# Seven products instead of eight for the gates and for half of u, with the tokens' sums stored ahead

## The chip, the core and the metric

The kernel runs on one core of a Trainium2 chip. The core has five engines that each work through their own list of instructions in order: TensorE (PE in the profile), VectorE (DVE), ScalarE (ACT), GpSimd (POOL) and SyncE (SP, which here issues DMA transfers). They meet only at semaphores. The metric is the device time of one execution in microseconds (us), the median of several runs.

## The reference

The kernel computes one decoder block for 2048 tokens of 1024 channels, all in float32:

```
h    = rmsnorm(x)
proj = h @ w_in                     # 1024 -> 5376 columns
q, k, v = rope(..), rope(..), ..    # 12 heads of 64
u, z = gelu(..), gelu(..)           # 512 columns each
gate_a, gate_b = sigmoid(..), ..    # 1024 columns each
y_attn = dilated_attention(q, k, v) # 3 groups x 4 heads; softmax over the groups' log-sums
y_gmlp = u * (spatial(layernorm(z)))
y = (gate_a * (y_attn @ wa) + gate_b * (y_gmlp @ wg)) @ w_out
x = x + rmsnorm(y)
x = x + rmsnorm(relu(rmsnorm(x) @ w1)**2 @ w2)
```

The change concerns `proj` alone: the 2048 columns of the two gates for all tokens, and the 512 columns of u for the first 1024 tokens.

## The kernel before, in words

A float32 product is made of three products of numbers of fewer bits: each operand is split into a high part (a rounded copy) and a low part (the difference), and `mm3` (lines 95 to 97) adds high x high, high x low and low x high in one bank of PSUM. `split` (lines 70 to 78) makes the two parts: the high part is a copy on ACT (or POOL, line 72), the low part a subtraction on DVE. A "step" is the smallest piece of projection work that is placed by hand: one k block of 128 channels, three matmuls with 512 tokens in their free axis.

The tokens are four chunks of 512, chunks 0 and 1 being half 0, chunks 2 and 3 half 1. The program has these stages. The first part normalises x, transposes it into hT (`prenorm_cols`) and makes v, q and k. hT of two chunks lies in SBUF at a time (high and low, 4 MB for both): while the first part works on chunks 2 and 3, hT of 0 and 1 goes to memory in DRAM as `hT_d` and is read back later by `reload_h`. Then come u and z of half 1, and then the gates, of half 1 first and of half 0 after it. The gates' steps are the filler for attention: 48 attention units (three groups of 16) need PE for some 3 us each, in four short bursts that wait for other engines (scores; transposes of the exponentials; probabilities times v; transposes of the result), and between the bursts the main loop calls `steps(n)`, which takes n steps from the generator `filler`. In an attention unit ACT makes the exponentials (`e`, L585), copies the transposed ones out of PSUM (`ph` L610, `pf` L618) and copies the result (`pvs` L626); DVE subtracts the row maximum and takes the sums (`nm` L582, `o` L631). `att` holds the unnormalised results with their row sums.

When the last unit is through, `combine` joins the three groups, chunk by chunk: it loads A (L639), takes the maximum M, the exponentials E (L647) and the weights, multiplies (L659), adds (L661, L662, on DVE for the first chunk and POOL for the others), transposes on PE (`yt`, L667) and copies out. `steps(30)`, 20, 17 and 13 of filler stand ahead of the four transposes. Then u and z of half 0 are made, the two branches and the gates are merged, and the MLP follows, whose first matrix product (L994) is already done by Strassen's seven products, with the sums of its weights made on POOL (L965 to L968) from the raw tiles `w1r`, of which it holds five.

Nothing is scheduled by a planner around the change: each engine's order is the order of the program text as the generators interleave it, and every tile has a fixed number of buffers, for which the next user waits. SP's queue, too, is in order: a DMA that waits for a buffer or for its data holds back all those behind it.

## Time and profile before

| | us |
|---|---|
| three runs | 2790.17, 2791.38, 2792.4 (median 2791.38) |
| the profiled execution, its span | 2791.02, 2789.3 |
| first part (v, q, k), until | 431.6 |
| u of half 1, until | 475.3 |
| z of half 1, until | 525.8 |
| gates, attention units from 548.5, last unit's transposes at | 1017.7 |
| combine and u of half 0, until | 1098.8 |
| z of half 0, until | 1145.9 |
| branches and merge, until | 1493.9 |
| MLP | 2779 |

The stage times are starts of PE's instructions in the timeline. The profile shows for each instruction its engine, line, output and input tiles, shape, duration, and the idle time of its engine just ahead of it with what ended it. Matmuls are pipelined: one of 512 columns is shown with 0.39 us, but a new one starts about every 0.23 us, and that spacing is what counts. The mean granted clock of TensorE is 0.99 of full speed over the span.

### The profile page before, as it was taken

To read this page: it belongs to the slowest core of one execution; us is meant where nothing else is said; L and a number is where in the kernel's file an instruction comes from. 1 tells how busy PE (TensorE), PEld (TensorE's weight loads), DVE (VectorE), ACT (ScalarE), POOL (GpSimd) and SP (SyncE) were. 2 spreads that over 40 slices of the span, in tenths; PEclk is the share of its full clock that TensorE was granted. 3 is DMA by queue.
4 is the path that set the end of the run, shared out by engine and by line. 5 is a ranking of instruction groups with operands and counts; after the bars stand their busy time and mean duration, and the time that the engine had idled before them with its cause. 6 is when DMAs were issued, how large, how long until landed. Compare 5 with 4: busy or idle time off the path is not lost. (4 is left out here: it accounts for less than half of the span.)

```text
span 2789.3 us, 36260 instructions
## 1 busy us (share of the span) xinstructions
PE 2720.9 (98%) x13412; PEld 2282.3 (82%) x13412; DVE 1545.3 (55%) x2643; ACT 1053.1 (38%) x2151; POOL 945.3 (34%) x777
## 2 busy tenths in 40 slices
PE   8999999999989999999998999999999999999998
PEld 8889888988878888887787788788887887777787
DVE  5664562344443344564556644555436777777766
ACT  4212111144444321354444554555444333233334
POOL 0241341200000014312315432323214666777645
PEclk9999999999999999999999999999999999999999
DMA  7545446366666645555657544554343122222236
GB/s 256 177 147 165 155 148 198 113 190 197 193 204 195 195 162 163 158 193 163 185 181 250 169 117 129 170 178 121 109 143 114 54 83 84 83 83 84 83 104 213
DMA packets 298386, 426.10 MB, mean 153 GB/s; under 512 B 18528, under 2 KB 172384, under 8 KB 298208
## 3 DMA queue, kind: packets, MB, share of 16 engines
q1 hardware_dynamic: 210512, 372.64, 41.9%
q10 hardware_dynamic: 87696, 51.13, 6.1%
q8 instruction: 106, 1.74, 0.3%
...
## 5 line engine op out<-in xcount | busy, mean ns | idle before, releaser
L1534 PE MATMUL ya<-T_spots,s 128*128 128x512 f32 x1272 | 313.3, 392 | 4.7 <-DVE acc L1542 2.7
L1534 PEld LDWEIGHTS ya<-T_spots,s 128*128 128x128 f32 x1272 | 239.1, 188 | 59.1 <-issue 4.5
L70 ACT ACTIVATE s<-sraw 128x768 fp32r<-128x768 f32 (+1 forms) x184 | 126.2, 696 | 358.3 <-POOL sraw L1333 199.3
L994 PE MATMUL aa<-B,A 128*128 128x512 f32 x768 | 187.1, 396 | 6.8 <-ACT xs L1008 4.5
L78 DVE TENSOR_TENSOR s<-sraw,s 128x512 fp32r<-128x512 f32 x171 | 163.7, 980 | 34.8 <-ACT s L70 33.2
L994 PEld LDWEIGHTS aa<-B,A 128*128 128x128 f32 x768 | 145.3, 190 | 40.8 <-ACT xs L1008 4.9
L965 POOL TENSOR_TENSOR s<-w1r 128x512 f32<-128x512 f32 x32 | 43.1, 1348 | 395.5 <-DVE S L78 335.1
L72 POOL TENSOR_SCALAR w_g<-w_g_r 128x1024 fp32r<-128x1024 f32 x32 | 33.6, 1050 | 412.5 <-PE g L97 330.1
L1534 PE MATMUL yc<-T_spots,s 128*128 128x512 f32 x624 | 164.3, 394 | 3.6 <-POOL T_spots L78 3.6
L95 PE MATMUL x<-hT_a,wq 128*128 128x512 f32 x384 | 149.7, 390 | 0.0
L97 PE MATMUL x<-hT_a,wq 128*128 128x512 f32 x384 | 149.4, 389 | 0.0
L96 PE MATMUL x<-hT_a,wq 128*128 128x512 f32 x384 | 149.4, 389 | 0.0
L1534 PEld LDWEIGHTS yc<-T_spots,s 128*128 128x128 f32 x624 | 115.9, 188 | 33.7 <-POOL T_spots L78 9.7
L631 DVE TENSOR_REDUCE o<-po 128x256 f32<-128x512 f32 x48 | 33.2, 691 | 183.5 <-PE po L630 183.5
L78 POOL TENSOR_TENSOR T_spots<-w2r,T_spots 128x512 fp32r<-128x512 f32 x86 | 123.2, 1458 | 5.4 <-ACT T_spots L70 5.4
L70 ACT ACTIVATE hl<-r 128x512 fp32r<-128x512 f32 x48 | 30.4, 634 | 231.4 <-POOL r L276 86.7
L95 PE MATMUL g<-hT_b,w_g 128*128 128x512 f32 x256 | 105.6, 412 | 0.0
L95 PE MATMUL o<-wo,mg 128*128 128x512 f32 x256 | 100.9, 394 | 4.1 <-ACT mg L70 4.1
L95 PE MATMUL g<-hT_a,w_g 128*128 128x512 f32 x256 | 104.5, 408 | 0.0
L793 POOL TENSOR_TENSOR g<-g,g 128x512 f32<-128x512 f32 x28 | 38.8, 1385 | 185.7 <-DVE g L791 185.6
L70 ACT ACTIVATE S<-w1r 128x512 fp32r<-128x512 f32 x96 | 60.1, 630 | 110.0 <-PE ac L994 63.8
L97 PE MATMUL g<-hT_a,w_g 128*128 128x512 f32 x256 | 100.8, 394 | 0.0
...
## 6 DMA issues: line engine op xcount, KB each, us to landing
...
sraw<-sd SPq DMA_DIRECT2D x128, 256.0 KB, 3.4
qk<-hl SPq DMA_DIRECT2D x24, 1024.0 KB, 5.3
...
w2r<-in_w_mlp_out_dram SPq DMA_DIRECT2D x16, 1024.0 KB, 6.6
```

What stands on the lines that cost most here:

```text
L70: act.activation(hi, src, AF.Copy)
L72: pool.tensor_scalar(hi, src, 1.0, 1.0, op0=OP.mult, op1=OP.mult)
L78: (pool if lo_eng == "pool" else dve).tensor_sub(lo, src, f32(hi))
L95: pe.matmul(ps, lh, rh, start=start, stop=False)
L96: pe.matmul(ps, lh, rl, start=False, stop=False)
L97: pe.matmul(ps, ll, rh, start=False, stop=stop)
L631: dve.tensor_reduce(ot[:, :, j * 64:(j + 1) * 64], po.rearrange("p (b h e) -> p b e h", b=4, h=2), axis=AX.X, op=OP.add)
L793: (dve if dt == KT - 1 else pool).tensor_add(parts[0], parts[0], parts[1])
L965: pool.tensor_add(s1, a21, a22)
L994: pe.matmul(p, w[:, l, k, :], h[:, r, k, :], start=i in (1, 6, 5) and not k and not n, stop=k == 3 and n == 2, skip_group_check=True)
L1534: pe.matmul(p, s[:, l], w[:, r], start=i in (1, 2, 5) and not m and not o, stop=m == 1 and o == 2, skip_group_check=True)
```

## The change

The gates' weights are taken as pairs: 256 columns (two blocks f of 128), 1024 channels (two halves), against a half's 1024 tokens (two chunks). Such a pair is a 2 x 2 by 2 x 2 block product. Before it was 8 block products of 4 steps; now it is 7, by Strassen's scheme in Winograd's form, for the 16 gate pairs (those of half 1 first, then those of half 0) and for the two pairs of u of half 0. A pair has thus 28 steps (84 matmuls) where it had 32 (96). The A operands are the weights and their sums (A11, S2, A12, S3, S1, A22, S4), the B operands the tokens and their sums (B11, T2, B21, T3, T1, T4, B22), in this order of use.

- The sums of the tokens T1 to T4 are made in the first part: for each of the odd chunks and each block of 128 tokens, two reads of the even chunk's h from `h_d`, four subtractions on POOL, and one store into `t1_d`. ACT's extra copy of each transposed block, which half the chunks had, is now made for all.
- The sums of the weights are made pair by pair: one raw tile `wr` of 1 MB (one buffer) is loaded, four POOL operations over 128 x 512 make S1, S3, S2 and S4 in place, and each of the seven operands is split by ACT and DVE into one of four places of `A_room`. `prepare(m + 4)`, which does this for the operand of the product four places later, stands behind product m.
- The products' results are joined with two ACT copies (xs and c1) and five DVE additions a pair.
- Operands of half 1 lie in SBUF as they come from the first part (B) or are read ahead of the gates (T). During the last pair of half 1 each operand of half 0 takes the place of the one just used: `load_op`, two loads of 512 KB, two high parts on ACT and two low parts on DVE of 128 x 1024, 14 of each in place of `reload_h`'s 8.
- 16 gate pairs and 2 u pairs are 504 steps, where there were 576. The loop over attention units gives each unit 8 steps up to unit 25 and 9 later (it was 9 throughout), `combine` gets 24, 14, 9 and 5 steps. u and z of half 1 are now complete, with their `sz_out`, before the tiles of attention are opened.

The rows below are from the engines' lists of instructions: in brackets what a row waits for, x the count of like rows.

**SP's queue behind z of half 1, before.** `ygd` is the store of the spatial gating's result, `ur` the read of u that belongs to it, `w_g_r` the raw weights of a gate.

```order
L91 DMA w_g_r_4799<-in_w_in_dram 128x1024 [waits DMAHW7_49,DMAHW6_49,DVE_49]
L421 DMA ygd<-sb_4514 128x512 [waits Pool_49]
L421 DMA ygd<-sb_4525 128x512 [waits DMAHW0_49,Pool_49]
L414 DMA ur_4668<-ud 128x512 [waits DMAHW4_49,DMAHW1_49]
L414 DMA ur_4679<-ud 128x512 [waits DMAHW5_49,DMAHW2_49]
L91 DMA w_g_r_4804<-in_w_in_dram 128x1024 [waits DMAHW3_49,DVE_49]
L91 DMA w_g_r_5085<-in_w_in_dram 128x1024 [waits DMAHW6_49,DVE_49]
L479 DMA gated<-gt_4637 128x512 [waits Activation_49]
L91 DMA w_g_r_5090<-in_w_in_dram 128x1024 [waits DMAHW3_49,DVE_49]
```

**The same place now**; `wr` is a pair's raw weights, `gated` the store of a gate.

```order
L436 DMA ygd<-sb_4613 128x512 [waits DMAHW7_49,Pool_49]
L522 DMA wr_4700<-in_w_in_dram 128x2048 [waits DMAHW0_49,PE_49]
L429 DMA ur_4768<-ud 128x512 [waits DMAHW4_49,DMAHW1_49]
L436 DMA ygd<-sb_4756 128x512 [waits DMAHW2_49,Pool_49]
L429 DMA ur_4779<-ud 128x512 [waits DMAHW6_49]
L436 DMA ygd<-sb_4767 128x512 [waits Pool_49]
L429 DMA ur_4790<-ud 128x512 [waits DMAHW5_49,DMAHW1_49]
L436 DMA ygd<-sb_4778 128x512 [waits Pool_49]
L542 DMA gated<-c_2_4823 128x512 [waits DMAHW7_49,Activation_49]
L522 DMA wr_4842<-in_w_in_dram 128x2048 [waits DMAHW0_49,DVE_49]
L436 DMA ygd<-sb_4789 128x512 [waits Pool_49]
```

The first weights of the gates, which were asked for between the stores and waited only for their own buffer, are now one load of 1 MB that waits for PE (the tile lies where the weights of z were, which z's last matmul reads) and stands behind a store that waits for POOL; the second pair's waits for the first's low parts on DVE.

**ACT in one attention unit of the first group, before.** `gt` is the copy of a finished gate block.

```order
L477 ACTIVATE gt_5270<-g_5181 128x512 [waits DMAHW5_49,PE_49]
L610 ACTIVATE ph_5257<-pT_5252 128x512 [waits PE_49,Activation_49]
L585 ACTIVATE e_5223,o_4834<-e_5223,nm_5238 128x256 [waits DVE_49]
L585 ACTIVATE e_5223,o_4834<-e_5223,nm_5238 128x256 x3
L610 ACTIVATE ph_5265<-pT_5260 128x256 [waits PE_49,Activation_49]
L618 ACTIVATE pf_5268<-pT_5260 128x256 [waits DVE_49]
L626 ACTIVATE pvs_5301<-pv_5292 128x512 [waits PE_49,Activation_49]
```

**ACT in such a unit now**; the tile `A_room` receives the high parts of a pair's seven operands.

```order
L737 ACTIVATE ph_5708<-pT_5703 128x512 [waits PE_49,Activation_49]
L712 ACTIVATE e_5674,o_5383<-e_5674,nm_5689 128x256 [waits DMAHW2_49,DVE_49]
L70 ACTIVATE A_room<-wr_5657 128x512 [waits DMAHW7_49]
L712 ACTIVATE e_5674,o_5383<-e_5674,nm_5689 128x256 x3
L737 ACTIVATE ph_5716<-pT_5711 128x256 [waits PE_49,Activation_49]
L70 ACTIVATE A_room<-wr_5657 128x512 [waits PE_49,Pool_49]
L745 ACTIVATE pf_5719<-pT_5711 128x256 [waits DVE_49]
L753 ACTIVATE pvs_5749<-pv_5740 128x512 [waits PE_49,Activation_49]
L70 ACTIVATE A_room<-wr_5657 128x512 [waits PE_49]
```

Where a copy that waits for PE alone stood, there are now high parts. The first in these rows waits for the load of the next pair's raw tile and stands ahead of three exponentials and of `ph`; the second waits for POOL's sums and stands ahead of `pf` and `pvs`.

**DVE behind the last unit's sum, before**: the combine's first rows follow it at once (w_u is a filler weight).

```order
L631 TENSOR_REDUCE o_8545<-po_9132 128x4x64 [waits PE_49]
L78 TENSOR_TENSOR w_u_0_9408<-w_u_r_9409,w_u_0_9408 128x1024 [waits DMAHW0_49,Pool_49]
L78 TENSOR_TENSOR w_u_1_9413<-w_u_r_9414,w_u_1_9413 128x1024 [waits DMAHW2_49,Pool_49]
L642 TENSOR_TENSOR M_9148<-A_9144 128x16 [waits DMAHW1_49,DMAHW0_49]
L643 TENSOR_TENSOR M_9148<-M_9148,A_9144 128x16 [waits DMAHW2_49,DVE_49]
L646 TENSOR_TENSOR E_9151<-A_9144,M_9148 128x4x4 [waits DVE_49]
L646 TENSOR_TENSOR E_9151<-A_9144,M_9148 128x4x4 x2
L650 TENSOR_TENSOR Z_9156<-E_9151,A_9144 128x4x4 [waits Activation_49]
```

**DVE at the same place now**, starting three rows behind the last `o<-po`; `u_115`, `xs` and `u_113` are outputs of the first u pair, `w_z` the weights of z of half 0.

```order
L78 TENSOR_TENSOR A_room<-wr_9341,A_room 128x512 [waits PE_49,Activation_49]
L572 TENSOR_TENSOR u_115_9599<-xs_9548,s_113_9552 128x512 [waits DMAHW5_49,DVE_49,PE_49]
L78 TENSOR_TENSOR w_z_0_9453<-w_z_r_9454,w_z_0_9453 128x1024 [waits DMAHW7_49,Pool_49]
L78 TENSOR_TENSOR w_z_1_9458<-w_z_r_9459,w_z_1_9458 128x1024 [waits DMAHW6_49,DMAHW0_49,Pool_49]
L578 TENSOR_TENSOR u_115_9599<-u_115_9599,s_116_9608 128x512 [waits DVE_49,PE_49]
L769 TENSOR_TENSOR M_9480<-A_9476 128x16 [waits DMAHW2_49,DMAHW1_49]
L581 TENSOR_TENSOR xs_9548<-xs_9548,s_113_9552 128x512 [waits DMAHW6_49,PE_49]
L78 TENSOR_TENSOR w_z_0_9463<-w_z_r_9464,w_z_0_9463 128x1024 [waits DMAHW3_49,Pool_49]
L584 TENSOR_TENSOR u_113_9565<-u_113_9565,s_116_9608 128x512 [waits PE_49]
L78 TENSOR_TENSOR w_z_1_9468<-w_z_r_9469,w_z_1_9468 128x1024 [waits DMAHW4_49,Pool_49]
L770 TENSOR_TENSOR M_9480<-M_9480,A_9476 128x16 [waits DMAHW5_49,DVE_49]
L773 TENSOR_TENSOR E_9483<-A_9476,M_9480 128x4x4 [waits DVE_49]
```

Ahead of the first chunk's maximum M, or between its two halves, there are now four low parts of `w_z`, one of `A_room`, and four additions of the first u pair, which wait for PE's products.

The diff, cut to its core:

```diff
--- before.py
+++ after.py
-    hT_d = dtile([2, P, KT, 512], "hTd")
+    h_d = dtile([3, P, KT, 512], "hd")
+    t1_d = dtile([2, P, 4, 4, 512], "t1d")
...
     def prenorm_cols(c, i):
+        half, odd = c // 2, c % 2
         if i == 0:
-            hT[c] = hp.tile([P, 2, KT, 512], F32R, name=f"hT_a{c}", tag="hT", bufs=2)
-        h, xt = hT[c], xts.pop((c, i))
-        for k in range(0, KT, 4):
+            H[c] = [hp.tile([P, 2, 4, 512], F32R, name=f"B{n + 1}{odd + 1}_{half}", tag=f"B{n + 1}{odd + 1}") for n in range(2)]
+        xt, isl = xts.pop((c, i)), slice(i * P, (i + 1) * P)
+        raw = xp.tile([P, 5, 4, P], F32, name=f"tr_{c}{i}", tag="tr", bufs=2)
+        if odd:
+            for n in range(2):
+                sp.dma_start(raw[:, 3 * n], h_d[c - 1, :, 4 * n:4 * n + 4, isl])
+        for n in range(2):
+            k = 4 * n
...
-            hh, hl = (h[:, o, k:k + 4, i * P:(i + 1) * P] for o in range(2))
+            hh, hl = (H[c][n][:, o, :, isl] for o in range(2))
             p3 = pt.rearrange("p (k t) -> p k t", k=4)
             act.activation(hh, p3, AF.Copy)
             dve.tensor_sub(hl, p3, f32(hh))
-            if c < 2:
-                raw = xp.tile([P, 4, P], F32, name=f"hr_{c}{i}{k}", tag="hr", bufs=3)
-                act.activation(raw, p3, AF.Copy)
-                sp.dma_start(hT_d[c, :, k:k + 4, i * P:(i + 1) * P], raw)
-    def reload_h(c):
-        hT[c] = hp.tile([P, 2, KT, 512], F32R, name=f"hT_b{c}", tag="hT", bufs=2)
-        for k in range(0, KT, 2):
-            split_in(hT[c][:, :, k:k + 2], hT_d[c, :, k:k + 2, :], None, "act")
+            to = raw[:, 2 + 2 * n if odd else n]
+            act.activation(to, p3, AF.Copy)
+            if c < 3:
+                sp.dma_start(h_d[c, :, k:k + 4, isl], to)
+        if odd:
+            pool.tensor_sub(raw[:, 0], raw[:, 2], raw[:, 0])
+            pool.tensor_sub(raw[:, 1], raw[:, 4], raw[:, 0])
+            pool.tensor_sub(raw[:, 2], raw[:, 4], raw[:, 2])
+            pool.tensor_sub(raw[:, 3], raw[:, 3], raw[:, 1])
+            sp.dma_start(t1_d[half].rearrange("p o k t -> p (o k) t")[:, :, isl],
+                         raw[:, :4].rearrange("p o k t -> p (o k) t"))
...
+    SEVEN = ((1, "A11", "B11"), (6, "S2", "T2"), (2, "A12", "B21"), (7, "S3", "T3"), (5, "S1", "T1"), (4, "A22", "T4"),
+             (3, "S4", "B22"))
+    pairs = [(13 + n, gate_d, n, 1) for n in range(8)] + [(13 + n, gate_d, n, 0) for n in range(8)]
+    pairs += [(9, u_d, 0, 0), (10, u_d, 1, 0)]
+    ops = {}
+    def load_op(half, name):
+        pl = hp if name[0] == "B" else tp
+        w = pl.tile([P, 2, 4, 512], F32R, name=f"{name}_b{half}", tag=name)
+        if name[0] == "T":
+            src = t1_d[half, :, int(name[1]) - 1]
+        else:
+            k = 4 * (int(name[1]) - 1)
+            src = h_d[2 * half + int(name[2]) - 1, :, k:k + 4]
+        for k in (0, 2):
+            split_in(w[:, :, k:k + 2], src[:, k:k + 2], None, "act")
+        ops[half, name] = w
+    def seven():
+        seq = [(p, *t) for p in pairs for t in SEVEN]
+        room = hp.tile([P, 2, 4, 512], F32R, name="A_room", tag="B12")
+        left, raws = {}, {}
+        def prepare(m):
+            if m >= len(seq):
+                return
+            pair, i, name, _ = seq[m]
+            wi = pair[0]
+            if name == "A11":
+                raws["t"] = ap.tile([P, 2560], F32, name=f"wr_{m}", tag="wr")
+                sp.dma_start(raws["t"][:, :2048], a["w_in"][wi].rearrange("p k c -> p (k c)"))
+            t = raws["t"]
+            q = t[:, :2048].rearrange("p (k c) -> p k c", c=256)
+            a11, a12, a21, a22 = (q[:, k:k + 4, f:f + P] for f in (0, P) for k in (0, 4))
+            s1 = t[:, 2048:].rearrange("p (k c) -> p k c", c=P)
+            w = room[:, :, m % 4].rearrange("p o (k c) -> p o k c", k=4)
+            split(w[:, 0], w[:, 1], dict(A11=a11, S2=a11, A12=a12, S4=a12, S3=a21, S1=s1, A22=a22)[name])
+            left[m] = w
+            if name == "A11":
+                pool.tensor_add(s1, a21, a22)
+                pool.tensor_sub(a21, a11, a21)
+                pool.tensor_sub(a11, s1, a11)
+            elif name == "A12":
+                pool.tensor_sub(a12, a12, a11)
+        def put(pair, f, ci, t):
+            _, dst, n, half = pair
+            if dst is u_d:
+                act.activation(t, t, AF.Gelu_apprx_tanh)
+            c = 2 * half + ci
+            sp.dma_start(dst[2 * n + f, :, c * 512:(c + 1) * 512], t)
+        for m in range(4):
+            prepare(m)
+        for m, (pair, i, name, bn) in enumerate(seq):
+            half = pair[3]
...
+            w, h = left.pop(m), ops[half, bn]
+            for k in range(4):
+                for n, (l, r) in enumerate(((0, 0), (0, 1), (1, 0))):
+                    pe.matmul(p, w[:, l, k, :], h[:, r, k, :], start=i in (1, 6, 5) and not k and not n,
+                              stop=k == 3 and n == 2, skip_group_check=True)
+                yield
+            if i == 1:
+                xs = ap.tile([P, 512], F32, name=f"xs_{m}", tag="xs", bufs=2)
+                act.activation(xs, p, AF.Copy)
+            elif i == 2:
+                c1 = ap.tile([P, 512], F32, name=f"c1_{m}", tag="u", bufs=3)
+                act.activation(c1, p, AF.Copy)
+                put(pair, 0, 0, c1)
+            elif i in (6, 7):
+                u = ap.tile([P, 512], F32, name=f"u{i}_{m}", tag="u", bufs=3)
+                dve.tensor_add(u, xs, p)
...
+            elif i == 5:
+                dve.tensor_add(u7, u7, p)
+                put(pair, 1, 1, u7)
...
+            if half and pair[2] == 7:
+                load_op(0, bn)
+            prepare(m + 4)
+    def plain_0():
+        load_op(0, "B12")
...
+    ended = []
+    def filler():
+        yield from plain_1()
+        yield
+        yield from seven()
+        ended.append(True)
+        yield
+        yield from plain_0()
     fill = filler()
...
-    ez = ExitStack()
-    zps[1] = stack(ez, "zp1", 1)
+    etp, ez = ExitStack(), ExitStack()
+    tp = stack(etp, "tp", 1, side="right")
+    for name in ("T2", "T3", "T1", "T4"):
+        load_op(1, name)
+    for name in ("B11", "B21"):
+        ops[1, name] = H[2][int(name[1]) - 1]
+    ops[1, "B22"] = H[3][1]
+    zps[1] = stack(ez, "zp1", 1, side="right")
     e1b = ExitStack()
-    at1 = stack(e1b, "at1", 2, side="right")
     sg = spatial(zps[1], 1)
     next(sg)
     steps(72)
     next(sg)
+    steps(2 * 4 * 8 + 2 * 32 - 72 + 1)
+    ew1.close()
+    ap = stack(e1, "ap", 1)
+    sm = stack(e1, "sm1", 2)
+    steps(9)
+    sz_out(*late.pop(0))
+    ez.close()
+    at1 = stack(e1b, "at1", 2, side="right")
...
-    steps(2 * 4 * 8 + 2 * 32 + 16 - 72)
-    ez.close()
+    steps(8)
     at = stack(e1b, "at", 2, side="right")
     steps(12)
     for n in range(len(units) + 1):
-            steps(6 if n > 1 else 9)
+            steps(9 if n < 2 else 5 if n < 26 else 6)
...
+    n_w = 4
+    wp = stack(e1, "wp2", 2)
+    st = stack(e1, "st2", 1)
+    z_w = [load_w(11 + n, f"w_z{n}0") for n in range(2)]
     ec = ExitStack()
...
     for n in range(4):
-        steps((30, 20, 17, 13)[n])
+        steps((24, 14, 9, 5)[n])
...
     ec.close()
+    while not ended:
+        steps(1)
+    etp.close()
...
-    steps(48)
+    steps(32)
     next(sg)
     run(fill)
     e1.close()
```

60 lines of the change are left out of this document (39 added, 21 removed).

## The prediction

> **What bounds the kernel now.** The page's busy table comes first.
>
> ```profile
> span 2789.3 us, 36260 instructions
> PE 2720.9 (98%) x13412; PEld 2282.3 (82%) x13412; DVE 1545.3 (55%) x2643; ACT 1053.1 (38%) x2151; POOL 945.3 (34%) x777
> ```
>
> PE is busy 98% of the span, the others a third to a half, so a matmul taken away is time taken away, unless PE then stands for something that its own work covered. Which stages have such cover is seen in the view by stage; its columns are the stretch, its length, and busy time (count) of PE, weight loads, DVE, ACT, POOL, then clock, DMA share, GB/s.
>
> ```profile
> 12.00:431.60 419.60, 415.71 (x2425) 369.53 (x2425) 241.37 (x348) 94.69 (x204) 125.04 (x87) 0.99 0.52 171
> 548.50:766.00 217.50, 217.50 (x1267) 189.00 (x1266) 90.35 (x286) 98.57 (x298) 14.78 (x15) 1.00 0.65 194
> 766.00:805.30 39.30, 31.67 (x167) 26.41 (x166) 21.65 (x46) 20.49 (x48) 2.10 (x2) 0.94 0.69 229
> 1017.70:1098.80 81.10, 75.39 (x337) 62.20 (x336) 45.38 (x117) 16.25 (x27) 33.53 (x20) 0.96 0.68 221
> 1494.00:2138.00 644.00, 630.29 (x2706) 509.23 (x2705) 347.96 (x430) 337.52 (x551) 219.47 (x154) 0.99 0.48 149
> ```
>
> The gates under attention (548.5 to 766) leave PE no idle time at all. The two short stretches do: 766 to 805.3, where hT is read back, and 1017.7 to 1098.8, the combine. The last row is the MLP's first product, the same seven products already at work without attention beside them.
>
> Next the timeline, for the price of a matmul and of the read-back (columns: start, duration, engine, line, output<-input; in brackets the idle time ahead and its end).
>
> ```profile
> 599.66 0.39 PE L96 MATMUL g<-hT_a,w_g 128*128 128x512 f32 x1
> ...
> 601.95 0.39 PE L97 MATMUL g<-hT_a,w_g 128*128 128x512 f32 x1
> ```
>
> Eleven gate matmuls stand in these rows, ten intervals in 2.29 us: 0.229 us each.
>
> ```profile
> 758.91 0.69 DVE L631 TENSOR_REDUCE o<-po 128x256 f32<-128x512 f32 x1 [3.80 <-PE po L630]
> 768.22 0.69 DVE L631 TENSOR_REDUCE o<-po 128x256 f32<-128x512 f32 x1 [3.98 <-PE po L630]
> ...
> 808.92 0.69 DVE L631 TENSOR_REDUCE o<-po 128x256 f32<-128x512 f32 x1 [4.61 <-PE po L630]
> 818.97 0.69 DVE L631 TENSOR_REDUCE o<-po 128x256 f32<-128x512 f32 x1 [3.97 <-PE po L630]
> 796.47 1.06 ACT L70 ACTIVATE hT_b<-hT_b 128x1024 fp32r<-128x1024 f32 x1 [5.54 <-DMA hT_b<-hTd]
> 801.82 0.39 PE L624 MATMUL pv<-ph,v 128*128 128x256 f32 x1 [3.15 <-ACT ph L610]
> ```
>
> One such sum stands in every attention unit, so their distance is the unit's length: 9.31 us undisturbed (758.91 to 768.22), but 50.75 us for the four units from 768.22 to 818.97, which is 13.5 more. The last two rows tell how: ACT stood 5.54 us with the high part of hT that waited for a load, `ph` was queued behind it, and PE stood for `ph`. Nobody was too slow; ACT's queue is in order. This is the pattern on which most of my sum rests.
>
> **The change part by part.** The sum is made against the profiled execution, 2791.0 us (span 2789.3 and 1.7 around it); the median of the runs is 0.4 above.
>
> *Removed.* 18 pairs lose 12 matmuls each: 216 x 0.229 = **-49.5**. The read-back's stalls go: **-13.5**.
>
> *The first part.* 32 subtractions on POOL over 128 x 512, 16 more copies on ACT, stores and reads on SP. The stretch 12 to 431.6 has POOL busy 125 of 420 us and ACT 95, so they lie beside PE's work; I take **+1**. If the stores behind POOL held up SP's loads it could be 4; if nothing is late, 0.
>
> *The durations of the new work* come from the MLP's groups, which do the same operations on the same shapes (sum, then mean in ns), and from the table of DMAs (count, KB, median us from issue to landing).
>
> ```profile
> L70 ACT ACTIVATE S<-w1r 128x512 fp32r<-128x512 f32 x96 | 60.1, 630 | 110.0 <-PE ac L994 63.8 <-POOL s L965 34.8 <-ACT xs L1004 4.2
> L78 DVE TENSOR_TENSOR s<-sraw,s 128x512 fp32r<-128x512 f32 x171 | 163.7, 980 | 34.8 <-ACT s L70 33.2 <-DMA out_dram<-acc_yt 1.3
> L965 POOL TENSOR_TENSOR s<-w1r 128x512 f32<-128x512 f32 x32 | 43.1, 1348 | 395.5 <-DVE S L78 335.1 <-DVE S L85 36.7 <-DMA w1r<-in_w_mlp_in_dram 23.8
> L78 DVE TENSOR_TENSOR hT_b<-hT_b 128x1024 fp32r<-128x1024 f32 x8 | 9.8, 1226 | 7.2 <-ACT hT_b L70 7.0
> v<-vd SPq DMA_DIRECT2D x9, 1024.0 KB, 5.4
> w2r<-in_w_mlp_out_dram SPq DMA_DIRECT2D x16, 1024.0 KB, 6.6
> 526.93 2.56 SPq L421 DMA_DIRECT2D ygd<-sb  x2
> ```
>
> *The start of the seven products.* In the order of SP's queue the first `wr` waits for z's last matmul (525.8) and stands behind a store that the last row here shows issued with its neighbour by 529.5. So wr is issued some 3 us behind z, lands 5.4 to 6.6 later, and A11's parts take 0.63 + 0.98: PE stands about 10 us, where the gates followed z with no gap. S2 needs three sums on POOL, 4.0 us, that overlap A11's product (2.7 us) only partly: +1.5. The second wr and the first attention loads stand in SP behind further stores that wait for POOL or DVE: +3.5. I take **+15**; 10 if only the first wait shows, 20 if the later ones double.
>
> *A pair under attention.* A product is 4 steps, half a unit of 8 steps: with units of 9.31 - 3 x 0.229 = 8.6 us it lasts 4.3. There is one raw tile, and its last reader is S4's split, which needs the place in A_room that product A12·B21 frees. From that product's end: S4's parts and their turn in the queues 1.7 to 4 us, the load 5.4 to 6.6, three sums 3 x 1.35 = 4.0; S2's high part is ready at 11.7 to 15.3 us (with 0.63). Its product is due 5 x 4.3 = 21 us after, so no product is late. But in ACT's queue A11 stands ahead of exponentials and `ph`, S2 ahead of `pf` and `pvs`, and in the pair shown in the order PE comes to that `pf` after 33 products' matmuls (7.6 us), one unit's bursts (9.31 - 27 x 0.229 = 3.1) and the next one's first products with v (some 0.7): 11.4 us. So PE stands up to 3.8 us there: the read-back's mechanism, once per pair. Where the unit's burst falls earlier or later against the pair (28 steps are 3.5 units, so two alignments alternate) ACT's next row is due later and the stall is nearer 1 or nothing. Over the 14 pairs that lie under attention I take 1.75 us each, a little under half of 3.8: **+25**. The low end is from the MLP: 2706 matmuls x 0.229 are 619.7 of its 644 us, 24 us over 32 pairs or 0.76 a pair, with five raw tiles and no attention; x 18 = 14. The high end is 14 x 3.8 = 53.
>
> The Trainium skill, DMA: Bandwidth & Descriptors (Anatomy of one DMA), puts a transfer at about 2.0 us plus its bytes by 436 GB/s, for DMAs that GpSimd issues: an estimate of 4.4 us for wr, and a sum some 10 us smaller. The rows here show 5.4 and 6.6 for the same size, and I go by them. Against the change speaks the Trainium skill's SBUF — State Buffer (Who interferes with whom): a DVE instruction with two SBUF inputs contends with a GpSimd instruction that reads SBUF, and every low part of the weights is one. The MLP's 1.35 us, measured beside such low parts, would already hold that.
>
> *The half switch.* In before 8 pieces of hT (a load, an ACT and a DVE row each) cost 13.5 us, 1.7 a piece. Now there are 14, each with a load that waits for the product that frees its place, in one pair of 4 units. At the old price they cost 23.6. DVE has 14 x 1.23 + 7 x 0.98 = 24 us in that pair beside attention's own part, in 35 us, so some of it must be late; but an operand is due only a whole pair after its place is free, so it may be late without harm where no attention row is behind it. Low end 4, **+15** taken.
>
> *The combine.*
>
> ```profile
> 1018.03 0.69 DVE L631 TENSOR_REDUCE o<-po 128x256 f32<-128x512 f32 x1 [7.27 <-PE po L630]
> 1029.46 0.17 DVE L642 TENSOR_TENSOR M<-A 128x16 f32<-128x16 f32 x1 [5.64 <-DMA A<-att]
> 1033.09 4.11 DVE L659 TENSOR_TENSOR A<-A,E 128x256 f32<-128x256 f32 x12
> 1039.69 1.06 PE L667 MATMUL yt<-ident,A 128*128 128x128 f32 x8 [1.26 <-issue]
> 1081.08 1.97 PE L667 MATMUL yt<-ident,A 128*128 128x128 f32 x8 [4.45 <-POOL A L662]
> ```
>
> From the last unit's sum to the first yt are 21.7 us, to the last 63, and the last still waited for POOL. PE had 80 steps of filler there, 80 x 0.687 = 55. Now it has 52, 35.7 us and some 3 for yt itself: 39. If the chain is as long as before, PE stands 63 - 39 = 24, where the stage before shows 5.7 idle: +18. DVE's rows of the u pair and of w_z ahead of M lengthen the chain (+6), buffers that come free earlier with fewer steps shorten it (-5): **+18**, from 13 to 24.
>
> *The rest*: seven products alternate two PSUM banks and wait for DVE's additions, which gates did not: **+2**, 0 to 4.
>
> Sum: -63 + 1 + 15 + 25 + 15 + 18 + 2 = +13, so 2791.0 + 13 = **2804**. All low ends give -63 + 10 + 14 + 4 + 13 = -22, 2769; all high ends -63 + 4 + 20 + 53 + 24 + 24 + 4 = +66, 2857.
>
> **The rivals.** *One, the matmuls decide.* The MLP's row is the best evidence: same sums, same engines, 0.76 us a pair. ACT is busy only 98.6 of 217.5 us under attention, POOL 14.8, so the new work fits by volume, and queues that drift apart may hide what places in the order seem to show. Against it: the MLP has five raw tiles and no `pf` behind them. All four waits near their low ends: 2769, faster.
>
> *Two, no change.* Pairs as in the MLP (14) but start, switch and combine as I take them: 2791 - 63 + 1 + 15 + 14 + 15 + 18 + 2 = 2793, within what can be told apart. By the 4.4 us load of the Trainium skill (DMA: Bandwidth & Descriptors, Anatomy of one DMA) it would be close to this too.
>
> *Three, the pairs decide alone.* If S2's wait for POOL meets `pf` in every pair, as in the pair shown, each costs 3.8: 53 in place of 25 gives 2832. It is decided by whether POOL's third sum ends more than 11.4 us behind A12·B21.
>
> *Four, the work is not saved.* If the new stage ran at more than 0.262 us per matmul (0.229 x 8/7) the seven products would give nothing, 2840 with the rest. The MLP's 644/2706 = 0.238 speaks against it.
>
> **How the numbers follow.** My forecast has 0.42 (2797 to 2828), rival one 0.36, two 0.14, three and four 0.08 together. About 0.2%, 5.6 us, is what can be told from no change here. So faster 0.36, same 0.14, slower 0.50. The likeliest time is 2804; the range goes from 2767, just below the sum of low ends, to 2832, rival three.
>
> **What would show it.** PE idle behind z's last matmul ahead of A11's product, 10 us or more. ACT rows A_room waiting for DMA wr and POOL wr under attention, and PE waiting for ACT at pv or po in most pairs; the sum o<-po every 8.6 to 8.9 us where nothing waits, with single units 2 to 4 us longer. Four long units at the half switch. PE idle ahead of yt of some 24 us in all. All my terms lie ahead of z of half 0, which started at 1098.8: I expect it near 1112. I am wrong if units keep 8.6 to 8.9 us throughout (then the pairs' term falls), or if z of half 0 starts earlier than before (then the matmuls decide).

## The result, and the profile after

The changed kernel takes 2839.5 us (median; 2837.8 to 2842.3), the kernel before 2790.9 us on the same chip: a ratio of 1.0174, 95% interval 1.0157 to 1.0192. It is 48.6 us slower; 13 were forecast, and the time lies above the range that was given.

One sentence ahead of the prediction has to be corrected. It says that nothing schedules the engines' rows around the change. That holds for PE alone: the rows of ACT, DVE, POOL and SP stand in an order that a scheduler makes, as the rows of the orders themselves show (the combine's M and E are written ahead of the filler's steps, and stand behind rows of the u pair). The prediction was made from the orders, so its steps do not hang on that sentence, but edits below move rows at places that nobody wrote down.

Where the time is. The starts of the same instructions in both traces bound five stages; a matmul of 512 columns that waits for nothing counts 0.228 us.

| stage, by PE's starts | before | after | matmuls fewer | time added beside them |
|---|---|---|---|---|
| start to u of half 1 | 431.8 | 437.6 | 0 | +5.8 |
| u and z of half 1 | 94.0 | 93.9 | 0 | 0 |
| end of z to the last unit's transposes | 491.9 | 536.5 | 69 | +60.3 |
| from there to z of half 0 | 81.4 | 77.9 | 147 | +30.0 |
| z of half 0 to the end | 1680.0 | 1681.3 | 0 | +1.3 |

The last column sums to 97.4 us, the 216 matmuls are 49.2 less, and 48.2 is what the spans differ by. The page after shows the same as less PE and more of everything else.

```profile
span 2837.5 us, 36367 instructions
PE 2697.8 (95%) x13196; PEld 2254.6 (79%) x13196; DVE 1695.6 (60%) x2839; ACT 1131.5 (40%) x2283; POOL 1054.2 (37%) x845
```

By stage (stretch, length, then busy time and count of PE, weight loads, DVE, ACT, POOL; clock, DMA share, GB/s) the rows that answer to those shown of before are:

```profile
11.00:437.60 426.60, 419.60 (x2427) 371.92 (x2426) 254.94 (x348) 102.90 (x221) 170.79 (x120) 0.98 0.64 204
531.50:574.40 42.90, 27.71 (x122) 21.55 (x121) 21.38 (x32) 11.04 (x17) 19.01 (x14) 0.80 0.58 177
574.40:783.00 208.60, 196.14 (x1121) 168.87 (x1122) 117.85 (x324) 105.68 (x304) 32.90 (x24) 0.97 0.65 197
783.00:856.00 73.00, 58.93 (x289) 48.56 (x288) 48.67 (x105) 41.28 (x98) 10.35 (x7) 0.86 0.77 250
856.00:1068.00 212.00, 204.90 (x1081) 174.74 (x1081) 118.81 (x342) 101.20 (x294) 39.73 (x30) 0.99 0.55 171
1068.00:1146.00 78.00, 44.85 (x192) 35.54 (x189) 63.91 (x136) 24.62 (x39) 37.46 (x19) 0.84 0.71 232
```

Under attention PE now stands 12 of 209 us where it stood for nothing; at the half switch (783 to 856) 14 of 73; in the combine 33 of 78, with DVE busy 64. The waits that the prediction expected are all there. First the timeline at one pair under attention, on ACT, POOL, DVE and PE:

```profile
692.18 0.63 ACT L70 ACTIVATE A_room<-wr 128x512 fp32r<-128x512 f32 x1 [0.66 <-DMA wr<-in_w_in_dram]
692.86 0.60 ACT L753 ACTIVATE pvs<-pv 128x512 f32<-128x512 f32 x1
696.62 0.63 ACT L70 ACTIVATE A_room<-wr 128x512 fp32r<-128x512 f32 x1 [3.17 <-POOL wr L533]
695.30 1.29 POOL L533 TENSOR_TENSOR wr<-wr 128x512 f32<-128x512 f32 x1
697.28 0.69 DVE L78 TENSOR_TENSOR A_room<-wr,A_room 128x512 fp32r<-128x512 f32 x1 [2.61 <-ACT A_room L70]
697.89 0.68 DVE L758 TENSOR_REDUCE o<-po 128x256 f32<-128x512 f32 x1
698.63 0.66 PE L732 MATMUL pT<-ident,e 128*128 128x128 f32 x4 [1.97 <-DVE o L758]
```

S2's high part waits 3.17 us for POOL's third sum, its low part holds DVE for 2.61, the sum `o` of the unit stands behind that, and PE waits 1.97 for the bank that `o` empties. So the stall does not only go through ACT to `pf`, as forecast, but also through DVE to the next transposes, five times between the first unit and the last. Ahead of the half switch the sums `o<-po` stand 8.0 to 9.0 us apart, and once in each pair 11 to 13: here 752.36 to 764.29.

```profile
743.75 0.69 DVE L758 TENSOR_REDUCE o<-po 128x256 f32<-128x512 f32 x1
752.36 0.69 DVE L758 TENSOR_REDUCE o<-po 128x256 f32<-128x512 f32 x1
764.29 0.68 DVE L758 TENSOR_REDUCE o<-po 128x256 f32<-128x512 f32 x1
```

Then the four transposes of the combine, and PE at the start of the seven products:

```profile
541.00 5.93 PE L560 MATMUL s<-B,A_room 128*128 128x512 f32 x12 [9.21 <-ACT A_room L70]
1097.26 1.94 PE L794 MATMUL yt<-ident,A 128*128 128x128 f32 x8 [12.50 <-issue]
1113.96 1.97 PE L794 MATMUL yt<-ident,A 128*128 128x128 f32 x8 [2.83 <-POOL A L789]
1124.93 1.10 PE L794 MATMUL yt<-ident,A 128*128 128x128 f32 x8 [1.69 <-POOL A L789]
1144.33 1.97 PE L794 MATMUL yt<-ident,A 128*128 128x128 f32 x8 [14.83 <-POOL A L789]
```

From the last unit's transposes (1068.0) the last yt comes after 76.3 us; before it was 63.4. Below, "chain" is this distance, and "PE's loss" of a stretch is, summed over its matmuls, the time from each start to the next less the spacing of its width when nothing waits (0.227 us for 512 columns, 0.118 for 256, 0.110 for 128). Attention's stretch loses 26.7 us before (13.5 of them the read-back) and 67.3 after; the combine 7.2 and 39.2. Five kernels below that leave attention's stretch almost as it is (a_four, wz_later, bare_tail, bare_and_wz_last, no_token_sums) lose 71 to 75 there in their profiles, so a difference of a few us between two profiles says nothing.

### The profile page after: what moved, and what is told of

The parts are those of the page before. It is cut to its first block, busy times and chain, and to the rows that moved or that the text cites. A ratio compares the mean times of both kernels' runs of the same rounds, so it can differ in the third digit from the quotient of the medians.

```text
span 2837.5 us, 36367 instructions
## 1 busy us (share of the span) xinstructions
PE 2697.8 (95%) x13196; PEld 2254.6 (79%) x13196; DVE 1695.6 (60%) x2839; ACT 1131.5 (40%) x2283; POOL 1054.2 (37%) x845
## 5 line engine op out<-in xcount | busy, mean ns | idle before, releaser
L560 PE MATMUL s<-T_b,A_room 128*128 128x512 f32 x864 | 228.7, 406 | 1.3 <-DVE A_room L78 0.7
L560 PEld LDWEIGHTS s<-T_b,A_room 128*128 128x128 f32 x864 | 160.4, 193 | 33.4 <-DVE A_room L78 1.4
L78 DVE TENSOR_TENSOR A_room<-wr,A_room 128x512 fp32r<-128x512 f32 x126 | 101.4, 808 | 117.8 <-ACT A_room L70 113.7
L531 POOL TENSOR_TENSOR wr<-wr 128x512 f32<-128x512 f32 x18 | 24.4, 1353 | 360.6 <-DMA wr<-in_w_in_dram 352.3
L97 PE MATMUL x<-B,wq 128*128 128x512 f32 x384 | 150.7, 392 | 2.7 <-DVE wq L78 2.7
L95 PE MATMUL x<-B,wq 128*128 128x512 f32 x384 | 150.7, 393 | 0.7 <-POOL wq L72 0.7
L96 PE MATMUL x<-B,wq 128*128 128x512 f32 x384 | 150.4, 392 | 0.0
L70 ACT ACTIVATE A_room<-wr 128x512 fp32r<-128x512 f32 x126 | 78.0, 626 | 117.4 <-POOL wr L533 41.0
L1478 POOL TENSOR_TENSOR sraw<-sraw 128x256 f32<-128x256 f32 x56 | 41.5, 740 | 174.5 <-DVE s L78 160.2
```

The costliest lines, as they stand in the source:

```text
L70: act.activation(hi, src, AF.Copy)
L78: (pool if lo_eng == "pool" else dve).tensor_sub(lo, src, f32(hi))
L95: pe.matmul(ps, lh, rh, start=start, stop=False)
L96: pe.matmul(ps, lh, rl, start=False, stop=False)
L97: pe.matmul(ps, ll, rh, start=False, stop=stop)
L531: pool.tensor_add(s1, a21, a22)
```

## Experiments

All ratios are to the kernel before, measured in the same job; the changed kernel stands at 1.0174.

**The pairs under attention.** The first run changes the order of POOL's sums alone.

```diff
                 pool.tensor_add(s1, a21, a22)
-                pool.tensor_sub(a21, a11, a21)
                 pool.tensor_sub(a11, s1, a11)
+                pool.tensor_sub(a21, a22, a11)
```

> POOL makes S2 as its second sum instead of its third (S3 is then made from A22 and S2), everything else as in the changed kernel. Theory A (S2's high part, which waits for POOL's third sum, stands in ACT's queue ahead of attention's rows, and that is what a pair costs): the waits of ACT's A_room rows for POOL get shorter by one sum, about 1.6 us each, and PE's waits of 2.1 to 2.7 us per pair under attention fall by about as much, so the stretch of attention gets some 15 to 20 us shorter: about 2822. Theory B (the pairs are long because the raw tile is loaded late, or because DVE has more to do than it can): a sum that comes earlier changes little, 2835 to 2840.

Measured: 2823.6 us, 1.0131 (1.0102 to 1.0161). Under attention ACT's waits for S2's sum fall from 35.3 to 23.8 us in all, attention's loss from 67.3 to 54.8. The earlier sum is worth about 12 us: theory A, a little under the 15 to 20 that it expected, because POOL now waits for A11's low part, which must have read S2's place (13.1 us in 14 waits).

The next takes both operands off the queues that attention uses, which is the undoing of the suspected cause.

```diff
+            engs = ("pool", "pool") if 7 <= m < 112 and name in ("A11", "S2") else ("act", "dve")
-            split(w[:, 0], w[:, 1], dict(...)[name])
+            split(w[:, 0], w[:, 1], dict(...)[name], *engs)
```

> S2 as POOL's second sum as in swap_s2, and both parts of A11 and S2 made on POOL for the 15 pairs behind the first, so that no ACT or DVE row waits for the raw tile's load or for S2's sum. Theory A (the pairs' loss is attention's rows queued on ACT and DVE behind these two operands): the pairs under attention lose less than 1 us each, attention's stretch gets another 10 to 15 us shorter than in swap_s2, about 2811 where swap_s2 had 2823.6. Theory B (what is left comes from the volume of ACT's and DVE's work or from the half switch): within 4 us of swap_s2, or longer where POOL's extra 4 us per pair make S2 late.

Measured: 2804.8 us, 1.0062 (1.0030 to 1.0093), theory A by more than it expected. The pairs' stalls are gone, though POOL has 4 us more to do in each. PE's waits from the first unit to the last, by what they waited for (engine, line, total, times, longest), are in the changed kernel

```profile
PE pT L732 <- DVE o L758: 12.0, 5, 4.4
PE pv L751 <- ACT pf L745: 6.8, 5, 2.1
PE po L757 <- ACT pvs L753: 6.6, 5, 2.5
PE pv L751 <- DVE ph L738: 6.0, 4, 3.4
```

and with the parts on POOL

```profile
PE pT L733 <- DVE o L759: 4.3, 1, 4.3
PE pv L752 <- DVE ph L739: 3.0, 2, 2.2
PE pv L752 <- ACT pf L746: 2.5, 3, 1.3
PE po L758 <- ACT pvs L754: 0.3, 1, 0.3
```

Attention's loss is 36.9. What is left of the waits lies at the half switch: the stretch behind it has PE busy without a gap.

```profile
780.00:850.00 70.00, 64.32 (x350) 54.19 (x350) 48.17 (x114) 40.76 (x106) 20.00 (x16) 0.95 0.72 227
850.00:1035.00 185.00, 184.63 (x980) 158.46 (x979) 99.10 (x299) 83.47 (x249) 61.55 (x53) 1.00 0.58 185
```

So the pairs cost 67.3 - 36.9 = 30 us, and what cost it is shown: two operands that wait for the load and for POOL, in queues that attention needs. This run also takes two high and two low parts a pair off ACT and DVE altogether, so less work there has a share that it does not part from the waiting; swap_s2, which moves no row off them, shows the waiting alone.

**The half switch.**

```diff
     def load_op(half, name):
+        if not half and name != "B12":
+            ops[half, name] = ops[1, name]
+            return
```

> Leaves out part of the computation: half 0's gates, u and z are made with half 1's operands (but for one block), so the 12 loads with 12 high and 12 low parts of 128 x 1024 that the half switch adds are gone; products, sums and stores stay. Theory A (the switch costs what its stretch shows above other pairs, about 20 us): attention's stretch gets 17 to 23 us shorter, about 2818. Theory B (the switch pair is long for the same reason as all pairs): 3 us or less.

Measured: 2824.3 us, 1.0134 (1.0096 to 1.0172); attention's loss 56.9. Taking the loads away gains 10 to 18 us of loss (against 67.3 in the changed kernel and 71 to 75 in the others) and about 11 of time, less than theory A's 17 to 23 or at most its low end, and far more than B: the stretch of the switch had pairs' stalls in it too. In parts_pool, without those stalls, the 50 us around the loads (764 to 814) still lose 18.0. Two edits tried to find the queue through which it goes.

```diff
-            split_in(w[:, :, k:k + 2], src[:, k:k + 2], None, "act")
+            split_in(w[:, :, k:k + 2], src[:, k:k + 2], None, "act" if half else "pool")
```

> The high parts of half 0's operands at the half switch are made on POOL instead of ACT, nothing else changes. no_switch_loads gained about 10 us against the changed kernel. Theory A (ACT's rows that wait for these loads ahead of attention's rows are the cost): 5 to 9 us of it are gained. Theory B (DVE's 14 low parts of 1.23 us beside attention's own work are the cost): within 3 us of the changed kernel.

Measured: 2841.4 us, 1.0187 (1.0157 to 1.0217), attention's loss 67.6: nothing gained. Theory B by elimination, and the next run tested it on top of parts_pool:

```diff
-            split_in(w[:, :, k:k + 2], src[:, k:k + 2], None, "act")
+            split_in(w[:, :, k:k + 2], src[:, k:k + 2], None, "act", "dve" if half or k else "pool")
```

> On top of parts_pool, one of the two low parts of each of half 0's operands is made on POOL instead of DVE. Moving the high parts off ACT gained nothing, so DVE is the suspect. Theory A (DVE's 14 low parts are the cost of the switch): PE's waits of 11 us at the switch fall by 4 to 8 us. Theory B (the loads' arrival blocks both queues whatever is queued there): less than 2 us, or more where POOL then delays S2.

Measured: 2810.9 us, 1.0082 (1.0064 to 1.0102), attention's loss 39.9 against 36.9: nothing gained (all_four below, which has the same edit, loses 35.9). Each edit relieves one queue in part, this one by 7 of DVE's 14 low parts. The traces say where the waiting went. In the 64 us around the loads PE waits in parts_pool 7.3 us for DVE's rows (`o`, `ph`) and 2.8 for ACT's; in switch_half 4.3 for DVE's and 5.1 for ACT's; in switch_pool, where ACT was relieved and the pairs' stalls are still there, 11.7 for DVE's and 1.6 for ACT's. So what one queue gives up the other takes, as far as these rows show; no run relieved both, and the first row that holds the others stays open.

**The first part.**

```diff
-            pool.tensor_sub(raw[:, 0], raw[:, 2], raw[:, 0])
-            (three more, two reads of h_d, the store into t1_d)
-            src = t1_d[half, :, int(name[1]) - 1]
+            src = h_d[2 * half, :, :4]
```

> Leaves out part of the computation: the token sums T1 to T4 are not made and not stored (no reads of h, subtractions or stores for them in the first part); the T operands are read from h instead. Theory A (these rows delay the splitting of wq, the first part's 5.8 us): u of half 1 starts at about 433 instead of 437 to 439. Theory B (the 16 extra copies and stores of h do it): no change in that start.

Measured: u of half 1 starts at 432.0, as before (431.8), against 437.6; 2835.2 us, 1.0165 (1.0135 to 1.0194). Theory A. In the changed kernel PE waits for the first weights of q, 3.4 us at one place. Their high parts stand on POOL behind a subtraction that waits for a DMA:

```profile
92.19 1.30 POOL L226 TENSOR_TENSOR tr<-tr 128x512 f32<-128x512 f32 x1 [6.80 <-DMA hd<-tr]
93.46 2.06 POOL L72 TENSOR_SCALAR wq<-wq_r 128x1024 fp32r<-128x1024 f32 x2
98.03 0.80 PE L97 MATMUL x<-B,wq 128*128 128x512 f32 x1 [2.74 <-DVE wq L78]
```

POOL's queue is not all of it. In all_four (below) these high parts are made on ACT, and PE still waits 2.05 us at this place for the low part on DVE. In both kernels ACT stands more than 6 us just ahead for a load of x (6.67 and 6.40), and DVE's rows for that x stand ahead of the low parts; in no_token_sums ACT has no such wait there. SP's queue with the sums' reads and stores is thus the second suspect. The run took reads, subtractions and store away together, so their shares are not told apart.

**The start of the seven products**, on top of parts_pool:

```diff
-                sp.dma_start(raws["t"][:, :2048], ...)
+                (sp if m else act).dma_start(raws["t"][:, :2048], ...)
-            sp.dma_start(dst[...], t)
+            (act if pair is pairs[0] and not f and not ci else sp).dma_start(dst[...], t)
```

> On top of parts_pool, the first raw tile is asked for on ACT's queue, so it no longer stands behind a store that waits for POOL, and the first output of the first pair is stored from there too. Theory A (SP's queue costs some 3 us of the 9.4 us that PE stands behind z, and some of the wait for attention's first operands): the stall behind z falls to about 6.5 us, the start in all by 3 to 5 us. Theory B (the wait for z's last matmul and the load itself are all of it): no change, 9 us or more.

Measured: 2806.7 us, 1.0067 (1.0047 to 1.0087). From z's last matmul to the first product it takes 7.0 us in place of 10.8, as theory A said, and to attention's first scores 39.4 in place of 42.1; but the whole does not differ from parts_pool. The wait for z's last matmul and the load make the larger part. A first raw tile that lies elsewhere could be loaded during z; that was not tried.

**The combine.** Six runs asked what makes its 30 us.

```diff
-            steps(9 if n < 2 else 5 if n < 26 else 6)
+            steps(9 if n < 2 else 5)
-        steps((24, 14, 9, 5)[n])
+        steps((30, 20, 17, 8)[n])
```

> Every attention unit from the third on gets 8 steps, and the 23 steps that are saved so stand ahead of the combine's transposes: 30, 20, 17 and 8 where the changed kernel has 24, 14, 9 and 5. Theory A (the combine's chain is a latency that has to be covered, PE stands for its length less the steps there): PE's waits ahead of yt fall from 30 us by up to 23 x 0.687 = 16 us, the units of the third group lose at most a few us: about 2825. Theory B (the chain is stretched because the filler's own rows on ACT, DVE and POOL stand between its links): more filler stretches it further, the waits ahead of yt fall by less than 6 us: 2834 or more.

Measured: 2838.3 us, 1.0184 (1.0154 to 1.0213). The combine's loss falls by 8 us to 31.4, half of the 16 of cover: the chain grew to 84.5. The time shows no gain, but 8 us lie within its interval, and attention's loss of 73.8 is no more than that of kernels that keep their steps. Neither theory whole: filler made of seven products was here half cover and half load.

```diff
-    z_w = [load_w(11 + n, f"w_z{n}0") for n in range(2)]      # ahead of the combine
+    z_w = [load_w(11 + n, f"w_z{n}0") for n in range(2)]      # behind its first six loads
```

> The weights of z of half 0 are asked for behind the combine's first six loads instead of ahead of them. Theory A (in the changed kernel the third load of the first A stands in SP's queue behind a load of w_z that waits for its buffer, and so the first yt comes 7 us later than before): the first yt comes 6 to 8 us earlier against the last unit's sum, PE's wait ahead of it falls from 12.5 us to about 5, and the whole by about 5 us: 2834. Theory B (E waits in ACT's queue behind the gelus of u, whose products come when they come): the first yt moves by less than 3 us, 2837 to 2840.

Measured: 2856.0 us, 1.0247 (1.0218 to 1.0277), worse by 20, which neither theory expected. The first yt comes 26.5 us after the last unit's transposes in place of 29.3, which is theory B's size, and the second 30 us after the first in place of 17: the weights' rows stood there instead. A second try asked for them behind the second yt, on top of parts_pool.

```diff
+        if n == 1:
+            z_w = [load_w(11 + n, f"w_z{n}0") for n in range(2)]
```

> On top of parts_pool, the weights of z of half 0 are asked for behind the combine's second yt, so that none of their loads stands in SP's queue between A's loads and none of their rows on POOL and DVE ahead of the first two chunks. Theory A (in the changed kernel the chain to the first yt is 7 us longer than before because of w_z: A's third load behind w_z's, low parts ahead of M): from the last unit's transposes to the first yt 22 to 25 us in place of 31, PE's loss in the combine from 42 down to 34 or less. Theory B (the u pairs' own rows and gelus do it): 29 us or more.

Measured: 2811.6 us, 1.0085 (1.0064 to 1.0105). The first yt comes after 24.2 us, 7 earlier than in parts_pool: theory A holds for the first link. But the chain is 81.3 long, where that of parts_pool is 78.9, and the loss 44: what was gained ahead of the first yt was lost ahead of the later ones.

```diff
+            left[m] = w
+            if pair[1] is u_d:
+                return
             split(w[:, 0], w[:, 1], ...)
```

> Leaves out part of the computation: the last two pairs (u of half 0) make no A operands (no load, no sums, no parts), their products take what lies in A_room; products, additions and gelus stay. Theory A (the combine's chain is longer than before because the filler's rows for A operands stand between its links on DVE, POOL and ACT): from the last unit's sum to the last yt it takes about 65 us instead of 76, and PE's loss from there to the last yt falls from 39 to about 28. Theory B (the rows of w_z and the gelus, or the transfers' own length, set it): 73 us or more.

Measured: 2834.1 us, 1.0161 (1.0127 to 1.0195); chain 71.5, loss 34.3. The operands' rows are 5 us of the chain, between the theories.

The forecast's own arithmetic was put to the test in the kernel before, whose filler is plain:

```diff
-        steps((30, 20, 17, 13)[n])
+        steps((24, 14, 9, 5)[n])
```

> The kernel before with 24, 14, 9 and 5 steps of its plain filler ahead of the combine's transposes instead of 30, 20, 17 and 13; the 28 others come behind them. If the forecast's arithmetic holds (a chain of 63 us less 39 us of cover): PE loses about 24 us between the last unit's transposes and the last yt, 7 before, so 2789 + 17 = about 2806. If the chain gets shorter with fewer steps, because buffers come free earlier: 10 to 15 us, 2795 or less.

Measured: 2799.4 us, 1.0034 (1.0014 to 1.0053), 10.3 us slower. The loss goes from 7.2 to 17.8, and the chain shrinks from 63.4 to 55.9 us. So fewer steps cost about 10 us by themselves, not 18. The other 20 of the changed kernel's 30 come from a chain that is 20 us longer with this filler.

```diff
+            left[m] = w
+            if pair[1] is u_d:
+                return
+        if n == 1:
+            z_w = [load_w(11 + n, f"w_z{n}0") for n in range(2)]
```

> Leaves out part of the computation: the last two pairs make no A operands, as in bare_tail; and the weights of z of half 0 are asked for behind the second yt, as in wz_last. If these two make up the difference: the chain is again about 63 us long, PE loses 24 to 28 us there instead of 39. If the gelus and the four additions a pair are the cause: 70 us or more, 33 us or more.

Measured: 2832.4 us, 1.0161 (1.0131 to 1.0191); chain 70.6, loss 33.4. So operands and w_z do not make the difference together either, and the second alternative is met: with them gone, the additions of the u pair, its gelus and the next weights remain between the links. The last chunk's rows in this run, on DVE from its maximum M to the multiplications and two of POOL beside them,

```profile
1118.47 1.91 DVE L772 TENSOR_TENSOR M<-A 128x16 f32<-128x16 f32 x1 [0.32 <-DMA A<-att]
1120.31 0.67 DVE L581 TENSOR_TENSOR u<-u,s 128x512 f32<-128x512 f32 x1
1120.43 2.34 POOL L792 TENSOR_TENSOR A<-A 128x1024 f32<-128x1024 f32 x1
1120.91 1.90 DVE L773 TENSOR_TENSOR M<-M,A 128x16 f32<-128x16 f32 x1
1122.74 2.06 POOL L72 TENSOR_SCALAR wb<-wbraw 128x1024 fp32r<-128x1024 f32 x2
1122.84 1.99 DVE L776 TENSOR_TENSOR E<-A,M 128x16 f32<-128x16 f32 x3
1126.12 0.69 DVE L584 TENSOR_TENSOR xs<-xs,s 128x512 f32<-128x512 f32 x1 [1.29 <-PE s L563]
1126.72 0.34 DVE L780 TENSOR_TENSOR Z<-E,A 128x16 f32<-128x16 f32 x3
1126.98 1.22 DVE L78 TENSOR_TENSOR wb<-wbraw,wb 128x1024 fp32r<-128x1024 f32 x1
1128.12 0.17 DVE L781 TENSOR_TENSOR M<-Z 128x16 f32<-128x16 f32 x1
1128.20 1.22 DVE L78 TENSOR_TENSOR wb<-wbraw,wb 128x1024 fp32r<-128x1024 f32 x1
1129.34 0.17 DVE L782 TENSOR_TENSOR M<-M,Z 128x16 f32<-128x16 f32 x1
1129.42 0.68 DVE L587 TENSOR_TENSOR u<-u,s 128x512 f32<-128x512 f32 x1
```

answer to these in before_52_steps:

```profile
1059.55 0.17 DVE L643 TENSOR_TENSOR M<-M,A 128x16 f32<-128x16 f32 x1
1059.76 0.34 DVE L646 TENSOR_TENSOR E<-A,M 128x16 f32<-128x16 f32 x3
1060.41 0.34 DVE L650 TENSOR_TENSOR Z<-E,A 128x16 f32<-128x16 f32 x3 [0.31 <-ACT E L647]
1060.70 0.17 DVE L651 TENSOR_TENSOR M<-Z 128x16 f32<-128x16 f32 x1
1060.91 0.17 DVE L652 TENSOR_TENSOR M<-M,Z 128x16 f32<-128x16 f32 x1
1061.72 4.11 DVE L659 TENSOR_TENSOR A<-A,E 128x256 f32<-128x256 f32 x12
```

From the chunk's maximum to its multiplications it takes 12.1 us there (1118.5 to 1130.6) and 4.2 here (1057.5 to 1061.7). Of these 7.9 us more, 3.4 lie in two links of the chain itself: the second M takes 1.90 us in place of 0.17 and E 1.99 in place of 0.34, each beside a row of POOL (the last section comes back to this). The low parts of `wb`, the next weights, take 2.3, and the u pair's additions, one of which waits for PE's product, the rest. The whole chain is 14.7 us longer than in before_52_steps: 4.9 by the time the last chunk starts, these 7.9, and 1.9 between its multiplications and its yt. The gelus on ACT have little part in it: they make ACT load a table of 1.28 us five times in the changed kernel's combine (three times before), but the exponentials of E start there within 0.4 us of the DVE rows that they need; in bare_and_wz_last one of the four starts 1.7 us late, in before_52_steps one 1.4.

**A in four buffers.** Chunks three and four are loaded only when one and two have been transposed. With four buffers all loads go out at once; the weights of z wait until the combine is through, since the room is needed.

```diff
-        A = cb.tile([P, 4, 3, 264], F32, name=f"A_{c}", tag="cA", bufs=2)
+        A = cb.tile([P, 4, 3, 264], F32, name=f"A_{c}", tag="cA", bufs=4)
-    for n in range(2):
+    for n in range(4):
         next(cs[n])
         next(cs[n])
-        steps((24, 14, 9, 5)[n])
+        steps((30, 6, 3, 3)[n])
```

> The changed kernel with A in four buffers: all twelve loads of the combine go out at once, the weights of z of half 0 are asked for behind it, and of the 52 steps 30, 6, 3 and 3 stand ahead of the transposes and 10 behind. Theory A (two buffers make the chain: chunks three and four are loaded only after one and two are transposed): from the last unit's transposes to the last yt 45 to 55 us in place of 76, z of half 0 starts some 20 us earlier, 2815 to 2820. Theory B (DVE's and POOL's work for four chunks beside the last pairs' is what takes the time): 70 us or more, 2835 or more.

Measured: 2854.4 us, 1.0233 (1.0212 to 1.0253). The chain is 11 us shorter (from 1074.1 to 1138.9), between the theories, and nothing is won: the last pair's raw tile stands behind twelve loads of A, and PE waits for its first operand.

```profile
1101.15 1.22 PE L560 MATMUL s<-B_b,A_room 128*128 128x512 f32 x2 [10.27 <-ACT A_room L70]
1117.03 3.93 PE L560 MATMUL s<-B_b,A_room 128*128 128x512 f32 x10 [14.65 <-DVE A_room L78]
```

The combine loses 34 us, and z of half 0 another 20 for its late weights. On top of parts_pool it was no better:

> parts_pool with the same edit. Theory A: the two repairs touch different stretches and add up: 2804.8 - 20 = about 2785, a little under the kernel before. Theory B: within 5 us of parts_pool.

Measured: 2818.1 us, 1.0104 (1.0087 to 1.0121), 0.4% above parts_pool. In the kernel before, the same edit (with 40, 14, 13 and 13 steps) found a plain filler:

> The kernel before, with A in four buffers and 40, 14, 13 and 13 steps ahead of the transposes. PE stood 5.7 us in this stretch before, so Theory A gives up to 6 us, 2783 to 2788; a chain that is covered by filler gains nothing by being shorter.

Measured: 2780.2 us, 0.9969 (0.9959 to 0.9979), 9 us **faster than the kernel before** and the fastest version of all. The combine's loss is 0.3 us, 7 less than before, with PE busy throughout. The edit also moves steps ahead of the first transposes (40 of the 80, where 30 stood), and no run parts the two.

```profile
1016.10:1074.80 58.70, 58.62 (x276) 48.64 (x275) 41.53 (x112) 10.09 (x19) 22.77 (x12) 1.00 0.63 210
```

**The repairs together.** all_four is parts_pool with wz_last, start_act, switch_half and the first wq's high parts on ACT; best_of_all is parts_a_four with start_act and those high parts.

> parts_pool with the three edits above together, and with the first wq's high parts on ACT, where POOL's subtractions for the token sums stand ahead of them. By the sum of theories A: 2804.8 - 7 (w_z) - 4 (start) - 6 (switch) - 4 (wq) = about 2784, that is even with the kernel before or a little faster; by theories B: within 5 us of parts_pool.

> parts_a_four with the first raw tile asked for on ACT's queue (gained 3.6 us behind z in start_act) and the first wq's high parts on ACT. If these hold: 4 to 6 us less than parts_a_four, about 2780, faster than the kernel before by 0.3%. If they are lost elsewhere: as parts_a_four.

Measured: 2806.2 us, 1.0067 (1.0050 to 1.0084), and 2815.0 us, 1.0092 (1.0077 to 1.0107). So all_four is within 5 us of parts_pool, and best_of_all 3 us below parts_a_four. all_four gains 4 us behind z and 1 in the first part, and gives them back in the combine (44.4); in best_of_all the first part gains nothing. No version of the seven products came out ahead of the kernel before: the best, parts_pool, is still 0.6% behind it.

## Why the prediction was right and wrong

The direction was right (slower), and the waits it rests on are in the trace. The sum was too small by 35 us; by its terms:

- *Removed, -49.5 and -13.5.* Right: 216 matmuls fewer, and no wait for hT.
- *The first part, +1 (0 to 4).* It cost 5.8. The step "they lie beside PE's work" looked at POOL's and ACT's share of the stretch and not at what stands behind the new rows in the queues: the first wq on POOL and, it seems, a load of x in SP's, which the term held at 4 at most. no_token_sums gives all of it back.
- *The start, +15 (10 to 20).* It cost 19.4: 9.4 of waiting behind z as worked out, 3.3 because the products after that wait follow one another more slowly, which no term held, and some 6.6 up to the first unit, 4.8 of them a wait for attention's first load.
- *A pair, +25 (14 to 53).* It cost 30 by this profile, a few us more by those of the other kernels. The mechanism was right to the operand: S2's sum in swap_s2, both operands in parts_pool. Its second way, through DVE to `o` and the next transposes, was not seen, and it is why pairs at both alignments cost something, 2 us in the mean, rather than one 3.8 and the other little.
- *The half switch, +15 (4 to 24).* It cost 10 to 18.
- *The combine, +18 (13 to 24).* It cost 30, 12 us more than taken and beyond the range given for it, and this is the step that failed. "If the chain is as long as before, PE stands 63 - 39" was wrong twice. With fewer steps and plain filler the chain gets shorter (before_52_steps: 56 us, 10 of loss). And the rows that lengthen it were put at +6, with buffers that come free earlier at -5, where the chain came out 20 us longer than with 52 plain steps. The prediction priced the rows that stand ahead of M once; they stand between the links of all four chunks, and links beside rows of POOL take longer themselves.
- *The rest, +2 (0 to 4).* Some 4 to 6: a median spacing of 231 ns against 229 under attention, and 1.3 behind it.

Against the 48 us that the spans differ by, these terms have to make up 111 (48.2 and the 49.2 and 13.5 removed); they add to 99 to 109, so 2 to 12 us are assigned to none of them.

Of the rivals, four named the measured time almost to the microsecond (2840), and that is luck. Its condition did not come true: the products follow one another every 0.231 us in the median, far from 0.262. Nor does its 2840 come out of the prediction's own terms, since it leaves out the 13.5 us of the read-back and the last term: 2791 - 13.5 + 1 + 15 + 15 + 18 + 2 gives about 2828. Rival three (2832, the pairs alone) was not what happened either: the pairs cost 30, not 53. Rival one was wrong in its evidence: the MLP's 0.76 us a pair did not carry over to attention, and shares of busy time that leave room say nothing of a queue in which rows wait. That the MLP has no short links on ACT and DVE beside its products is the likely reason; no run tested it. The 4.4 us that the prediction works out by the Trainium skill (DMA: Bandwidth & Descriptors, Anatomy of one DMA), from a fit for DMAs that GpSimd issues, are too short for these loads, which SP issues: `wr` took 6.2 us in the median, as the neighbouring rows of before had it.

The range was too narrow above. Every added term but the switch came out over the value taken. Most have a common cause, rows that wait in shared queues, so the range should not have counted on one being low when another is high.

Settled by runs: that the token sums cost the first part its time, the pairs' cost, and of the combine's 30 us the 10 that fewer steps cost and some 5 for the operands' rows. Only read from rows, and taken away by no run: that the u pair's additions, the low parts of `wb` and DVE's links beside rows of POOL make the remaining 15 us of the combine's chain. Open: how the first part's cost divides between the queues, and which row starts the waiting at the half switch.
